# First three weight blocks multiplied k tile by k tile, the first tiles of x^T loaded from another queue, and the last rows stored in four pieces

## The chip, the cores and the metric

One core of a Trainium2 chip runs the whole program. The time is that of one execution on the device, in microseconds (us); three executions of the kernel before gave 893.09, 893.13 and 894.57, median 893.13 us. PE is the matrix engine (TensorE), PEld its weight loads, DVE is VectorE, ACT is ScalarE, POOL is GpSimd, and SP is SyncE, which here does nothing but issue transfers (DMAs). ACT and POOL can issue DMAs too.

## What is computed

A decoder trunk of two layers on 256 rows of width 2048. In each layer the normalised rows are multiplied by an input projection, four head groups work on the parts of the product, their gated outputs are put side by side and multiplied by an output projection, and the result is added to the rows. A last normalisation ends it. All in f32; cut to what matters here:

```python
def hybrid_layer(x, ...):
    h = rms_norm(x, norm_g)
    p = split_columns(jnp.einsum("bsd,de->bse", h, w_in))
    ...
    mixed = jnp.concatenate([fox, diff, moba, gla], axis=-1)
    return x + jnp.einsum("bse,ed->bsd", mixed, w_out)

def reference(x, ...):
    for l in range(DEPTH):
        x = hybrid_layer(x, l, ...)
    return rms_norm(x, final_norm_g)
```

## The kernel before

**Tiling.** The 2048 inputs of a projection are 16 k tiles of 128. Weights are cut into blocks of up to 512 columns, and a block into steps of two or four k tiles, each a tile `raw` of at most 128 x 1024 f32; there are five such buffers, so the load of a sixth waits until the first is free. To keep f32 precision at the faster matmul type fp32r, every operand is split into a high part `hi` and a remainder `lo`: ACT writes `hi` (a rounding copy of `raw`), DVE then writes `lo` = `raw` - `hi`. The transposed rows x^T are split in the same way into `hTp` (high part and remainder for each k tile, scaled by the norm's gain `ngt`). A product is three matmuls for each k tile and half of the 256 rows: high x high, low x high and high x low, summed in PSUM. A `raw` buffer is free when its last `lo` has been written.

**The order.** A planner written in Python holds a list of steps (`plan`), issues the matmuls in that order and puts the other engines' work between them by its own estimates of time. Steps 0, 1 and 2 are the first two k tiles of three blocks of layer 0 (348, 512 and 348 columns; the third sums into a PSUM tile called `side`). They alone are loaded in halves of one k tile (`HALVED = 3`, line 38; lines 1551 to 1555). Steps 3, 4 and 5 are the next two k tiles of the same blocks, steps 6 and 7 and so on those after. x^T comes in four tiles `four` of four k tiles each; of the first the k tiles 0 and 1 are loaded one at a time, 2 and 3 together (`load_x`, line 1498), and the second (k tiles 4 to 7) is issued with step 6 (line 1544), behind the load of step 5, which takes the first freed `raw` buffer.

**The start.** `load` (line 1540) issues from SP, in turn: step 0's first half, x^T's k tile 0, step 0's second half, x^T's k tile 1, both halves of step 1, x^T's k tiles 2 and 3, both halves of step 2, and steps 3 and 4. ACT issues `ngt`, then loads its table and runs a small activation (line 1892). `parts_of` (line 1609) splits a halved step k tile by k tile; `split_xt` (line 1572) splits x^T, the first k tile's high part on DVE (`xt_hi`, line 1561), the others' on ACT. `multiply` (line 1812) issues for a halved step first the six matmuls of its first k tile, then the six of its second (line 1835). Before any of this PE multiplies ones, to have its clock up.

**The end.** For the last 256 columns the sums of the upper 128 rows are finished before those of the lower. `final_rows` (line 1438) then adds the residual, sums the squares, lets POOL raise the mean square to the power -1/2 (`rf`), and scales the rows: columns 1280 and up on ACT, with a store issued by ACT, the first 1280 columns on DVE in two pieces of 640, each with a store issued by SP.

## Time and profile before

| | |
|---|---|
| median of the three runs | 893.13 us |
| the profiled execution | 892.94 us |
| its span, first to last instruction | 891.2 us |
| PE busy | 881.5 us (99%) |
| DVE, ACT, POOL busy | 662.2, 559.1, 60.0 us |
| DMA moved | 227.45 MB, mean 255 GB/s |

The profiled execution lasted 1.74 us longer than its span. PE's busy time shows where PE had work under way, not how fast it was; the DMA share is the mean over the core's 16 DMA engines, and can come out a little over 1 in a short stretch.

### The profile page before, as it was taken

To read this page: it belongs to the slowest core of one execution; us is meant where nothing else is said; L and a number is where in the kernel's file an instruction comes from. 1 tells how busy PE (TensorE), PEld (TensorE's weight loads), DVE (VectorE), ACT (ScalarE), POOL (GpSimd) and SP (SyncE) were. 2 spreads that over 40 slices of the span, in tenths; PEclk is the share of its full clock that TensorE was granted. 3 is DMA by queue.
4 is the path that set the end of the run, shared out by engine and by line. 5 is a ranking of instruction groups with operands and counts; after the bars stand their busy time and mean duration, and the time that the engine had idled before them with its cause. 6 is when DMAs were issued, how large, how long until landed. Compare 5 with 4: busy or idle time off the path is not lost.

```text
span 891.2 us, 12456 instructions
## 1 busy us (share of the span) xinstructions
PE 881.5 (99%) x4380; PEld 750.8 (84%) x4380; DVE 662.2 (74%) x943; ACT 559.1 (63%) x846; POOL 60.0 (7%) x87
## 2 busy tenths in 40 slices
PE   9999999999999999999999999999999999999996
PEld 7988889888887888888899888898888888888886
DVE  6689878878867967656679778879676788585583
ACT  7577675577646667644756876578644575693461
POOL 1010110000110000000000100110000100101000
PEclk9999999999999999999999999999999999999999
DMA  8889897747988685977798898878958978499742
GB/s 289 294 263 303 266 301 241 254 147 263 288 240 274 203 317 178 362 265 228 235 302 265 285 320 224 253 227 277 337 147 262 301 220 271 168 301 363 236 143 96
DMA packets 84142, 227.45 MB, mean 255 GB/s; under 512 B 9979, under 2 KB 30443, under 8 KB 83950
## 3 DMA queue, kind: packets, MB, share of 16 engines
q1 hardware_dynamic: 73336, 192.00, 63.9%
q0 software_dynamic: 9152, 33.03, 14.5%
q10 hardware_dynamic: 1590, 1.62, 0.5%
q8 instruction: 34, 0.56, 0.3%
q14 instruction: 30, 0.25, 0.1%
HBM read 204.06 MB, written 22.55 MB: 254 GB/s over the span
## 4 chain that ended last, share of the span: by engine, by line
PE 93%; DVE 2%; DMA 2%; issue 1%; ACT 1%; SPq 0%; POOLq 0%; POOL 0%; DVEq 0%; ACTq 0%
PE mm L466 79%; PE side L466 14%; DMA raw<-in_weights 2%; DVE lo L466 1%; DVE four L466 1%; ACT hi L466 1%; DMA far<-four 0%; DVE mTl L466 0%; ACT four L466 0%; ACT L466 0%; DVE raw L466 0%; DVE eight L466 0%; SPq L466 0%; POOLq L1984 0%; POOL rf L466 0%
## 5 line engine op out<-in xcount | busy, mean ns | idle before, releaser
L466 ACT ACTIVATE hi<-raw 128x1024 fp32r<-128x1024 f32 (+2 forms) x319 | 316.6, 1011 | 190.9 <-PE mm L466 110.2
L466 PE MATMUL mm<-hi,hTp 128*128 128x512 f32 (+1 forms) x1760 | 432.7, 381 | 1.2 <-ACT hTp L466 0.9
L466 DVE TENSOR_TENSOR lo<-raw,hi 128x1024 fp32r<-128x1024 f32 (+2 forms) x319 | 363.7, 1157 | 93.3 <-ACT hi L466 89.0
L466 PEld LDWEIGHTS mm<-hi,hTp 128*128 128x128 f32 x1760 | 321.5, 188 | 60.3 <-ACT hi L466 1.3
L466 PE MATMUL mm<-lo,hTp 128*128 128x512 f32 (+1 forms) x880 | 237.4, 380 | 0.1
L466 PEld LDWEIGHTS mm<-lo,hTp 128*128 128x128 f32 x880 | 162.4, 188 | 30.6 <-DVE lo L466 0.8
L466 PE MATMUL mm<-hi,mTh 128*128 128x512 f32 (+1 forms) x256 | 69.3, 377 | 0.0
L466 PE MATMUL mm<-lo,mTh 128*128 128x512 f32 (+1 forms) x256 | 69.0, 376 | 0.1
L466 PE MATMUL mm<-hi,mTl 128*128 128x512 f32 (+1 forms) x256 | 69.0, 376 | 0.0
L466 PEld LDWEIGHTS mm<-lo,mTh 128*128 128x128 f32 x256 | 46.2, 188 | 9.2 <-DVE lo L466 0.5
L466 PEld LDWEIGHTS mm<-hi,mTl 128*128 128x128 f32 x256 | 46.3, 188 | 8.8
L466 PEld LDWEIGHTS mm<-hi,mTh 128*128 128x128 f32 x256 | 46.0, 188 | 8.6 <-ACT hi L466 0.4
L466 ACT ACTIVATE four<-mm,rstd 128x512 f32<-128x512 f32 (+2 forms) x56 | 36.7, 667 | 26.3 <-PE mm L466 26.3
L466 POOL DMA_DIRECT2D four<-far x40 | 21.8, 546 | 444.0 <-DMA far<-four 193.5
L466 DVE STREAM_TRANSPOSE four<-four 128x1024 f32<-128x1024 f32 (+1 forms) x34 | 39.1, 1149 | 6.7 <-ACT four L466 6.3
L466 ACT ACTIVATE four<-four 128x512 fp32r<-128x512 f32 (+3 forms) x44 | 35.5, 819 | 12.6 <-DMA four<-far 8.8
L466 PEld LDWEIGHTS side<-four,four 128*128 128x128 f32 (+1 forms) x336 | 37.7, 190 | 3.9 <-issue 1.8
L466 PE MATMUL side<-four,four 128*128 128x128 f32 (+3 forms) x336 | 39.3, 281 | 0.0
L1686 POOL DMA_DIRECT2D xs<-in_weights x24 | 21.2, 900 | 169.5 <-DVE lo L466 36.2
L466 DVE TENSOR_TENSOR lo<-xs,hi 128x1024 fp32r<-128x1024 f32 x24 | 29.1, 1214 | 1.8 <-ACT hi L466 1.8
L466 ACT ACTIVATE mTh<-four 128x1024 fp32r<-128x1024 f32 x16 | 16.9, 1057 | 21.2 <-DVE four L466 21.1
L466 ACT ACTIVATE hi<-xs 128x1024 fp32r<-128x1024 f32 x24 | 25.4, 1060 | 7.1 <-PE mm L466 6.2
(146 smaller groups left out, 685.1 us busy)
## 6 DMA issues: line engine op xcount, KB each, us to landing
raw<-in_weights SPq DMA_DIRECT2D x271, 512.0 KB, 4.9
four<-far POOLq DMA_DIRECT2D x34, 512.0 KB, 6.7
far<-four SPq DMA_DIRECT2D x128, 128.0 KB, 3.9
raw<-in_weights SPq DMA_DIRECT2D x46, 348.0 KB, 5.1
xs<-in_weights POOLq DMA_DIRECT2D x24, 512.0 KB, 8.5
xs<-in_weights SPq DMA_DIRECT2D x8, 512.0 KB, 8.3
xs<-in_x SPq DMA_DIRECT2D x4, 512.0 KB
kept<-xs SPq DMA_DIRECT2D x1, 2048.0 KB, 10.6
```

Of the source, the lines that this page charges most:

```text
L466: op.do()
L1686: g_.eng.dma_start(ys[:, c], weights[at:at + P * 1024].rearrange("(p j c) -> p j c", p=P, j=2), accum_op=OP.add)
```

## The change

The loads of the first three steps are put in another order: SP issues the first halves of the three, then their second halves, then x^T's k tiles 2 and 3. ACT issues x^T's k tile 0, `ngt` and x^T's k tile 1. ACT and DVE split, and PE multiplies, in that order too: all three blocks' k tile 0, then all three's k tile 1. The high part of x^T's k tile 1 is made by DVE instead of ACT. The three `raw` buffers come free one behind the other after the last of these halves. At the end DVE scales its 1280 columns in three pieces of 320, 448 and 512 columns instead of two, each with its store.

```diff
-        for i in range(2):
-            q = slice(i * 640, (i + 1) * 640)
+        for q in (slice(0, 320), slice(320, 768), slice(768, 1280)):
             v_.tensor_scalar(xs[:, m, q], xs[:, m, q], r, None, op0=OP.mult)
             nc.sync.dma_start(rows[:, q], xs[:, m, q])
...
         if i == 0:
+            load_x(nc.scalar, 0, 1)
             nc.scalar.dma_start(ngt, norm_gt)
+            load_x(nc.scalar, 1, 2)
...
         if i < HALVED:
-            for j in range(2):
-                nc.sync.dma_start(raw[:, j * n:(j + 1) * n], src[:, j * n:(j + 1) * n])
-                if i == 0:
-                    load_x(nc.sync, j, j + 1)
+            firsts.append((raw, src, n))
+            if i + 1 == HALVED:
+                for j in range(2):
+                    for to, part, m in firsts:
+                        nc.sync.dma_start(to[:, j * m:(j + 1) * m], part[:, j * m:(j + 1) * m])
+                load_x(nc.sync, 2, 4)
         else:
             q_.move(raw, src, LOADED)
-        if i == 1:
-            load_x(nc.sync, 2, 4)
...
-        if kt == 0:
+        if kt < 2:
             v_.tensor_scalar(hT[0][:, kt], src, g, None, op0=OP.mult)
...
-        for j in (slice(0, 1), slice(1, 2)):
-            hi_of(s["hi"][:, j], s["raw"][:, j])
-            if s is plan[0]:
-                split_xt((j.start,))
-            lo_of(s["lo"][:, j], s["raw"][:, j], s["hi"][:, j])
-        loads["freed"].append(times.of(s["lo"]))
+        if s is plan[HALVED - 1]:
+            for j in range(2):
+                for z in plan[:HALVED]:
+                    hi_of(z["hi"][:, j], z["raw"][:, j])
+                    if z is plan[0]:
+                        split_xt((j,))
+                    lo_of(z["lo"][:, j], z["raw"][:, j], z["hi"][:, j])
+            loads["freed"].extend(times.of(z["lo"]) for z in plan[:HALVED])
...
         if any(s is z for z in plan[:HALVED]):
-            products.sort(key=lambda z: z[2])
+            if s is plan[HALVED - 1]:
+                for j in range(2):
+                    for z in plan[:HALVED]:
+                        for x, part in ((lh, "hi"), (ll, "hi"), (lh, "lo")):
+                            for m in range(2):
+                                matmul(z["block"]["ps"][m][:, :z["block"]["n"]], x[:, z["kts"][j], m * P:(m + 1) * P], z[part][:, j],
+                                       j == 0 and x is lh and part == "hi", False, main=True)
+            return
         products = [(*z, m) for z in products for m in range(2)]
```

The first transfers on SP's queue in the kernel before: `raw` is weights (128x348 a half of step 0 or 2, 128x512 a half of step 1, 128x696 and 128x1024 whole steps), `four` is x^T, `x2` two in a row.

```order
L1553 DMA raw<-in_weights 128x348
L1501 DMA four_118<-in_xt 128x256
L1553 DMA raw<-in_weights 128x348
L1501 DMA four_118<-in_xt 128x256
L1553 DMA raw<-in_weights 128x512 x2
L1501 DMA four_118<-in_xt 128x512
L1553 DMA raw<-in_weights 128x348 x2
L466 DMA raw<-in_weights 128x696
L466 DMA raw<-in_weights 128x1024
L466 DMA raw<-in_weights 128x696
L1501 DMA four_175<-in_xt 128x1024
```

The same place on SP now:

```order
L1557 DMA raw<-in_weights 128x348
L1557 DMA raw<-in_weights 128x512
L1557 DMA raw<-in_weights 128x348 x2
L1557 DMA raw<-in_weights 128x512
L1557 DMA raw<-in_weights 128x348
L1500 DMA four_115<-in_xt 128x512
L466 DMA raw<-in_weights 128x696
L466 DMA raw<-in_weights 128x1024
L466 DMA raw<-in_weights 128x696
L1500 DMA four_169<-in_xt 128x1024
```

Step 1's first half has moved from fifth to second place, and the two single k tiles of x^T have left this queue. The last two rows, step 5's load and x^T's second tile, keep their places.

ACT's first instructions before:

```order
L1543 DMA ngt<-in_norm_gt 128x32
L1892 ACT_TABLE_LOAD
L1892 ACTIVATE halfpow<-halfpow 128x8
L466 ACTIVATE hi<-raw 128x348 x2
L466 ACTIVATE hTp<-four_118,ngt 128x256
L466 ACTIVATE hi<-raw 128x512 x2
```

ACT's first instructions now:

```order
L1500 DMA four_115<-in_xt 128x256
L1543 DMA ngt<-in_norm_gt 128x32
L1500 DMA four_115<-in_xt 128x256
L1902 ACT_TABLE_LOAD
L1902 ACTIVATE halfpow<-halfpow 128x8
L466 ACTIVATE hi<-raw 128x348
L466 ACTIVATE hi<-raw 128x512
L466 ACTIVATE hi<-raw 128x348 x2
```

Two DMA issues stand ahead of the table load, one of them ahead of `ngt`, and the activation on k tile 1 of x^T is gone from between the copies of `raw`.

PE's matmuls behind the ones, before; `mm_165` and `mm_166` are the PSUM tiles of the first block's two halves of the rows:

```order
L466 MATMUL mm_165<-hi,hTp 128x348
L466 MATMUL mm_166<-hi,hTp 128x348
L466 MATMUL mm_165<-hi,hTp 128x348
L466 MATMUL mm_166<-hi,hTp 128x348
L466 MATMUL mm_165<-lo,hTp 128x348
L466 MATMUL mm_166<-lo,hTp 128x348
L466 MATMUL mm_165<-hi,hTp 128x348
L466 MATMUL mm_166<-hi,hTp 128x348
```

And now; `mm_179` and `mm_180` are the second block's:

```order
L466 MATMUL mm_165<-lo,hTp 128x348
L466 MATMUL mm_166<-lo,hTp 128x348
L466 MATMUL mm_179<-hi,hTp 128x512
L466 MATMUL mm_180<-hi,hTp 128x512
L466 MATMUL mm_179<-hi,hTp 128x512
L466 MATMUL mm_180<-hi,hTp 128x512
L466 MATMUL mm_179<-lo,hTp 128x512
L466 MATMUL mm_180<-lo,hTp 128x512
L466 MATMUL side_181<-hi,hTp 128x348 x4
L466 MATMUL side_181<-lo,hTp 128x348 x2
```

Behind the six matmuls of the first block's k tile 0 now stand the six of the second block's k tile 0, then the third's. Behind these 36 matmuls, from step 3 on, the order on PE is the same in both.

## Rows read from the trace of the kernel before

**Rows 1.** What PE waited for over the whole span: waiting engine and tile, what ended the wait, us in total, times, longest.

```profile
PE mm L466 <- ACT hTp L466: 0.9, 1, 0.9
PE side L668 <- PEq L1977: 0.8, 1, 0.8
PE mm L466 <- DVE hTp L466: 0.2, 1, 0.2
```

**Rows 2.** Busy time of each engine by stage: the stretch and its length, busy us (and instructions) of each engine, the granted clock, the mean busy share of the DMA engines, GB/s.

```profile
4.32:6.70 2.38, 1.44 (x6) 0.90 (x6) 0.82 (x3) 0.92 (x2) 0.00 (x0) 1.00 0.96 312
6.70:12.76 6.06, 6.06 (x31) 5.19 (x31) 4.77 (x9) 4.68 (x9) 0.00 (x0) 1.00 0.99 369
12.76:883.64 870.88, 870.63 (x4338) 743.68 (x4336) 653.79 (x922) 550.59 (x832) 56.20 (x76) 1.00 0.80 256
883.64:891.20 7.56, 0.00 (x1) 0.00 (x0) 2.21 (x6) 0.94 (x1) 0.67 (x1) 0.82 0.38 144
```

**Rows 3.** The opening in order of time: start, us, engine, line, operation, output<-input, count, and in brackets idle time before it and what ended it. SPq and ACTq rows are DMA issues. Rows with a count are several instructions run together.

```profile
0.74 0.40 SPq L1553 DMA_DIRECT2D raw<-in_weights  x1
0.75 0.41 ACTq L1543 DMA_DIRECT2D ngt<-in_norm_gt  x1
...
1.19 1.28 ACT L1892 ACT_TABLE_LOAD   x1 [1.19 <-PEq L1977]
1.19 0.42 SPq L1501 DMA_DIRECT2D four<-in_xt  x1
...
1.67 0.42 SPq L1553 DMA_DIRECT2D raw<-in_weights  x1
...
2.49 0.21 ACT L1892 ACTIVATE halfpow<-halfpow 128x8 f32<-128x8 f32 x1
...
3.37 0.49 ACT L466 ACTIVATE hi<-raw 128x348 fp32r<-128x348 f32 x1 [0.67 <-DMA raw<-in_weights]
...
3.83 0.35 DVE L466 TENSOR_SCALAR hTp<-four,ngt 128x256 fp32r<-128x256 f32 x1 [2.89 <-DMA four<-in_xt]
...
4.32 1.01 PE L466 MATMUL mm<-hi,hTp 128*128 128x348 f32 x4 [0.19 <-DVE hTp L466]
...
5.18 0.58 PE L466 MATMUL mm<-lo,hTp 128*128 128x348 f32 x2
5.73 0.49 ACT L466 ACTIVATE hi<-raw 128x348 fp32r<-128x348 f32 x1 [1.87 <-DMA raw<-in_weights]
...
6.70 1.11 PE L466 MATMUL mm<-hi,hTp 128*128 128x348 f32 x4 [0.94 <-ACT hTp L466]
6.72 1.30 ACT L466 ACTIVATE hi<-raw 128x512 fp32r<-128x512 f32 x2
7.09 1.72 DVE L466 TENSOR_TENSOR lo<-raw,hi 128x348 fp32r<-128x348 f32 x3
...
8.05 0.43 SPq L1501 DMA_DIRECT2D four<-in_xt  x1
8.08 1.08 PE L466 MATMUL mm<-hi,hTp 128*128 128x512 f32 x4
...
10.85 0.79 PE L466 MATMUL side<-hi,hTp 128*128 128x348 f32 x4
...
12.76 1.44 PE L466 MATMUL mm<-hi,hTp 128*128 128x348 f32 x8
...
14.17 0.91 ACT L466 ACTIVATE hTp<-four,ngt 128x256 fp32r<-128x256 f32 x2 [0.47 <-DMA four<-in_xt]
...
17.13 0.77 ACT L466 ACTIVATE hi<-raw 128x696 fp32r<-128x696 f32 x1
...
19.33 1.41 PE L466 MATMUL mm<-hi,hTp 128*128 128x348 f32 x8
```

**Rows 4.** DMA issues of the first 20 us, and the last row from the page, over the span: output<-input, queue, count, KB each, median us from issue to landing.

```profile
four<-in_xt SPq DMA_DIRECT2D x2, 512.0 KB, 7.1
raw<-in_weights SPq DMA_DIRECT2D x4, 174.0 KB, 5.3
raw<-in_weights SPq DMA_DIRECT2D x2, 256.0 KB, 4.3
...
ngt<-in_norm_gt ACTq DMA_DIRECT2D x1, 16.0 KB, 2.8
...
xs<-in_weights SPq DMA_DIRECT2D x8, 512.0 KB, 8.3
```

**Rows 5.** The end in order of time, in the form of rows 3, and two stretches of it in the form of rows 2.

```profile
885.35 0.94 ACT L466 ACTIVATE xs<-xs,rf 128x768 f32<-128x768 f32 x1 [4.82 <-POOL rf L466]
885.36 1.02 DVE L466 TENSOR_SCALAR xs<-xs,rf 128x640 f32<-128x640 f32 x2 [0.45 <-POOL rf L466]
885.94 0.81 SPq L1455 DMA_DIRECT2D out<-xs  x2
886.32 0.38 ACTq L1451 DMA_DIRECT2D out<-xs  x1
...
886.72:888.00 1.28, 0.00 (x0) 0.00 (x0) 0.00 (x0) 0.00 (x0) 0.00 (x0) 1.00 0.98 373
888.00:889.57 1.57, 0.00 (x0) 0.00 (x0) 0.00 (x0) 0.00 (x0) 0.00 (x0) 0.64 0.97 362
```

More of the change, by code (lines that the diff above doesn't have):

```diff
@@ L1483, in hybrid_trunk @@
         plan.append({**z, "block": b, "need": {(b["need"], b["l"], k // 4) for k in z["kts"]}})
-    xts = []
+    xts, firsts = [], []
     ys = xs.rearrange("p m d -> p (m d)").rearrange("p (c j n) -> p c j n", c=4, j=2)
@@ L1834, in multiply @@
         if any(s is z for z in plan[:HALVED]):
-            products.sort(key=lambda z: z[2])
+            if s is plan[HALVED - 1]:
[6 more added lines that the diff above has]
+            return
         products = [(*z, m) for z in products for m in range(2)]
-        if (s["first"] or s["last"]) and not any(s is z for z in plan[:HALVED]):
+        if s["first"] or s["last"]:
             products.sort(key=lambda z: z[4])
```

## The prediction

> **What bounds the kernel now.** I read first what PE waited for over the whole span [rows 1]. Three entries make 1.9 us, and one of them, the 0.8 before the first instruction, no kernel escapes. The others, 0.2 and 0.9, both wait for a high part of x^T. Then the stages [rows 2]: from 12.76 to 883.64 PE is busy for 870.63 of 870.88 us at a granted clock of 1.00, so whatever PE gains or loses before 12.76 should arrive unchanged at 883.64. There PE is done, and 7.56 us follow in which the last rows are scaled and stored. The change touches these two ends alone: the stretch up to 12.76, where step 3 begins, and the last 7.56 us. Last, both ends in order of time.
>
> In the opening [rows 3] the first block's k tile 0 is multiplied from 4.32 to 5.76 (5.18 and 0.58). Then PE stands for 0.94, until 6.70, though it has only the first block to go on with: the order wants that block's k tile 1, whose weights reach ACT at 5.73 (ACT had stood 1.87 for them), then comes ACT's 0.49 for the weights and its copy of x^T's k tile 1, behind them PE. At 6.70 the two k tiles of the first block are half done. The second k tile lasts until 8.08, 1.38 us for six matmuls of 348 columns, because PE keeps pace with `lo`. With everything there the same six cost less: block 2, of the same shape, takes 10.85 to 12.76 for both k tiles, so 0.955 each. Block 1, 512 wide, takes 8.08 to 10.85, so 1.385 each.
>
> **The change, the opening.** Nothing of PE's work is added or taken away: 36 matmuls before and after. What stands behind k tile 0 of block 0 is now k tile 0 of block 1, and only then come block 2's, and k tile 1 of all three. Call T the moment at which block 1 starts. If nothing is late behind it, step 3 starts at T + 1.385 + 0.955 + 0.955 + 1.385 + 0.955 = T + 5.635, where block 0's second k tile is now priced as block 2's, since its operands have 2.3 us more. Against 12.76 the gain is 7.125 - T.
>
> T has two conditions. PE has to be through with block 0's k tile 0: 5.76 if that starts at 4.32 as now. And block 1's weights must have landed (moment L), been copied by ACT, 0.65 (two in 1.30), and seen by PE, 0.04 (ACT's copy ends at 6.66, PE starts at 6.70): T = L + 0.69.
>
> The first condition moves a little. ACT now issues three DMAs, at 0.41 each with a pitch of 0.46 (SP's first two start at 0.74 and 1.19), so its table load starts at about 2.13 instead of 1.19, and with 1.28 and 0.21 ACT is free at about 3.64 instead of waiting until 3.37: +0.27 for the first weights' copy, which then ends at 4.13. `ngt`, issued second, goes out at 1.21; with its 2.8 from issue to landing [rows 4] it is there at 4.01, where now x^T ends the wait at 3.83. So DVE's first high part comes 0.18 later and PE starts at 4.50, and is through at 5.94. That is a cost of nothing as long as T is later, its cover being the wait for block 1's weights.
>
> L is what the trace does not show. Block 1's first half is issued second on SP, at 1.19 instead of 2.60. From below: the transfer that was issued at 1.19 landed at 3.83, x^T's k tile 0, half as large. From above: the two 256 KB halves took 4.3 in the median, which gives 5.5, and the slowest kind among the halves 5.3, which gives 6.49. The nearest row is the one with the same place in the line: step 0's second half was third of the weights and x^T tiles, issued at 1.67, and ended ACT's wait at 5.73. Block 1's half is again the third (step 0's first half and x^T's k tile 0 go out with it); it has 82 KB more, 0.26 us at 312 GB/s, and is issued 0.48 earlier. I take L = 5.75, so T = 6.44: PE stands from about 5.94 to 6.44, step 3 starts at 12.08, gain 0.68. The ends: T cannot be below 5.76, gain 1.36; with L = 6.49 it is a loss of 0.05.
>
> Is anything late behind T? Block 2's k tile 0 is wanted by PE at 7.83, its copy (0.49) must begin at 7.3, and it is issued at 1.67: even 5.3 lands it at 6.97. Block 0's k tile 1 is wanted at 8.78, issued at 2.13; 5.3 lands it at 7.43. The later ones have more room. DVE now also makes the high part of x^T's k tile 1, 0.35, in a place where it has about 1 us to spare. The wait that goes is thus replaced by a shorter one, of about 0.5, for weights instead of x^T.
>
> The Trainium skill speaks against part of this ("DMA: Bandwidth & Descriptors", section Issuing engines are not separate DMA queues): transfers issued by ACT and SP run on the same 16 DMA engines and interleave, and a second issuing engine saves only issue time. The DMA share of 0.96 before 6.70 [rows 2] agrees that these engines have no time to give. By that rule x^T's k tile 1, issued by ACT at 1.67 and not wanted before 8.78, goes partly ahead of block 1's weights; its 131 KB at 312 GB/s would make L 0.42 later, T 6.86 and the gain 0.26, which is the second rival.
>
> **The change, the end.** Of what follows 883.64, only what DVE's pieces release moves. From its start at 885.36 to SP's issue it takes 0.58 for 640 columns [rows 5]. DVE's 256-column scaling takes 0.35 [rows 3], so 320 columns are there some 0.16 earlier, an estimate along the line between these two. SP then issues at 885.78, 886.24 and 886.70 with its 0.46 pitch; ACT's stays at 886.32. The first data moved 0.78 after the first issue, at 886.72, and then the engines were busy (0.98 and 0.97) until 889.57: 1.05 MB in 2.85 us. The volume is unchanged, the start is 0.16 earlier, and the second piece follows as the first (164 KB, 0.44 us) ends. I take 0.1 of gain. Below: the pieces of 320 and 448 columns go at the 312 GB/s of the opening's short rows, and 0.39 MB then cost 0.19 more; or the last issue, 0.30 later than the present last, ends it 0.3 later. So -0.3 to +0.16. The upper 128 rows' stores go out 5.76 us earlier and touch nothing.
>
> The same page (section Rules for kernel authors) wants many small transfers put together into one; the piece of 164 KB is smaller than any store here. No row shows a 320-column store; by the rule the end loses, and the sum becomes 0.68 less up to 0.3.
>
> **Sum.** 0.68 + 0.10 = 0.78 us: the profiled execution's 892.94 would become 892.16. It lies 0.19 under the median of 893.13, on which the forecast stands: 892.35, rounded 892.4.
>
> **Rivals.** First, block 1 is there in time: the early transfers are held up by latency and not by bytes, and with two queues issuing at once block 1's half lands by 5.07. For it: the first two transfers landed 0.46 apart, just their issue pitch, 2.64 after issue. Against it: the third, issued at 1.67, took until 5.73, so 4.06. Then the gap on PE is gone, 1.36 + 0.16, 891.6.
>
> Second, the gain is swallowed: block 1's half lands after 6.2, because x^T's k tile 1 and `ngt` share the engines with it, or because it takes the 5.3 of the slow halves. PE then stands a whole us or more where it stood 0.94, and the opening comes out at 0.26 to -0.05. For it: the share of 0.96. Against it: with the 4.06 that the third transfer took, block 1's half would be there at 5.25. Time 893.0.
>
> Third, slower: the buffers. Step 0's `raw` is now free only after its second half's `lo`, behind those of blocks 1 and 2: PE wants that `lo` at 8.78 + 0.64, so about 9.2, where now it came at 7.6 (the first of the three `lo` that start at 7.09). SP's issue of step 5 waits for that, and behind it stands x^T's second tile, now issued at 8.05, then at 9.65. Step 6, at 12.08 + 6.57 = 18.65 (19.33 - 12.76), needs its copies, 0.91, and its own weights' copy behind them on ACT, 0.77: landing later than 16.97 makes PE wait, later than about 17.75 it costs the whole gain. With the 7.1 of its kind it lands at 16.75, just in time; with the 8.3 that 512 KB took elsewhere on SP at 17.95, and PE loses 0.98: 0.20 over the present time, 893.3, up to 893.7 with the worst end. Against it: now it landed at 14.17, 6.1 after issue, behind a queue of bytes (share 0.99), and with the same bytes ahead it would land near that again.
>
> That the change does not do what it says, the orders on SP, ACT and PE exclude.
>
> **How the numbers follow.** What the measurement can tell from no change is about 0.2%, 1.8 us: below 891.3 or above 894.9. The forecast (a gain of 0.4 to 1.1) has 0.55, the first rival 0.15, the second 0.20, the third 0.10. All of them lie within 0.2%. Only the first rival with an end better than I can price, or luck in the runs (one of the three before was 1.4 above the others), leaves it: faster 0.05, slower 0.03, same 0.92. The range of 891.4 to 893.7 takes in the first rival's 891.6 and the third's worst end, with 0.2 for the runs' spread below.
>
> **What would show it.** Right: block 1's 128x512 matmuls follow the first six of 348 columns, PE's wait before them is about 0.5 and is ended by ACT's copy of the weights, block 0's second k tile takes about 0.95, step 3 starts near 12.1, no new wait of PE before 883 and the last matmul near 883.0; the first store at the end is issued 0.4 after DVE's start. Wrong: a wait of 1 us or more before block 1 (second rival), none (first), or a wait at step 6 for x^T (third), or a last DMA byte later than 5.9 us after the last matmul (the end).

## The result, and the profile after

The changed kernel is slower: 899.82 us median of six runs (896.12 to 901.46) against 893.35 (893.09 to 894.57) for the kernel before on the same chip, ratio 1.0065, 95% interval 1.0044 to 1.0086. A second series on another chip gave 898.72 us (twelve runs, 896.93 to 904.33), ratio 1.0051 [1.0031, 1.0071]. Chips differ, so below each kernel is given as its ratio to the kernel before in the same session; 0.1% is 0.9 us.

The profiled execution took 896.12 us, the fastest of the six. Its span is 894.3 us, where it was 891.2. So the trace explains 3.1 us, and the other 3 or so of the median have to come from places that vary from run to run. Of the 18 executions of the changed kernel in the two series, the five with the lowest mean granted clock, 0.992 to 0.994, took 900.80 to 904.33 us, and the others, at 0.995 to 0.998, 896.12 to 900.91.

What PE waited for over the span, in the form of [rows 1]:

```profile
PE mm L466 <- ACT hi L466: 1.7, 2, 1.5
PE mm L466 <- DVE lo L466: 0.9, 1, 0.9
PE side L668 <- PEq L1987: 0.8, 1, 0.8
```

The waits for x^T's high part are gone, and others of 2.6 us stand in their place. They lie at two places, the opening and one that the prediction did not look at. First the opening, PE, in the form of [rows 3]:

```profile
5.59 1.50 PE L466 MATMUL mm<-hi,hTp 128*128 128x348 f32 x4 [1.45 <-ACT hi L466]
6.89 0.78 PE L466 MATMUL mm<-lo,hTp 128*128 128x348 f32 x2
7.47 1.91 PE L466 MATMUL mm<-hi,hTp 128*128 128x512 f32 x4
9.17 0.84 PE L466 MATMUL mm<-lo,hTp 128*128 128x512 f32 x2
9.85 0.79 PE L466 MATMUL side<-hi,hTp 128*128 128x348 f32 x4
...
14.06 1.44 PE L466 MATMUL mm<-hi,hTp 128*128 128x348 f32 x8
```

The order is the intended one, but the first matmul comes at 5.59 instead of 4.32, and six matmuls of 512 columns fill 7.47 to 9.85, 2.38 us instead of 1.385: the first four take 1.70 us, 0.43 from one start to the next, twice the 0.23 of the second block's k tile 1 later (11.74). Six of 348 columns at 9.85 take 0.95 again. Until about 9.7 PE ran at half pace. The matmuls of ones ahead of it had run at that pace too, in both kernels: their weight loads, one for each 512 columns, start 0.43 apart (1.16, 1.59, 2.01 and so on). Step 3 starts at 14.06, not 12.76. The view by stages, in the form of [rows 2], tells nothing of it; PE is busy throughout and the clock reads 1.00:

```profile
5.59:14.06 8.47, 8.47 (x36) 7.69 (x37) 6.75 (x13) 6.35 (x11) 0.00 (x0) 1.00 0.94 330
```

What was late for the first matmul, on ACT and DVE:

```profile
0.74 0.41 ACTq L1500 DMA_DIRECT2D four<-in_xt  x1
1.19 0.45 ACTq L1543 DMA_DIRECT2D ngt<-in_norm_gt  x1
1.67 0.45 ACTq L1500 DMA_DIRECT2D four<-in_xt  x1
...
4.00 0.49 ACT L466 ACTIVATE hi<-raw 128x348 fp32r<-128x348 f32 x1 [0.34 <-DMA raw<-in_weights]
4.83 0.63 ACT L466 ACTIVATE hi<-raw 128x512 fp32r<-128x512 f32 x1 [0.34 <-DMA raw<-in_weights]
```

```profile
5.09 0.35 DVE L466 TENSOR_SCALAR hTp<-four,ngt 128x256 fp32r<-128x256 f32 x1 [4.16 <-DMA ngt<-in_norm_gt]
```

PE's row names ACT, but ACT's copy for the first block was done at 4.49. The last thing to be ready was DVE's high part of x^T, at 5.44, and that had stood for `ngt`, which took 3.9 us from its issue at 1.19 where it took 2.8 [rows 4]. Both ACT copies of weights came early enough.

The second place lies between 38 and 51 us. ACT and its DMA issues there, before and after:

```profile
38.52 0.44 ACTq L466 DMA_DIRECT2D four<-in_gla_wa  x1
...
42.68 0.24 ACTq L466 DMA_DIRECT2D four<-in_gla_ba  x1
42.97 1.06 ACT L466 ACTIVATE four<-four 128x1024 f32<-128x1024 f32 x1 [3.26 <-DMA four<-in_gla_wa]
```

```profile
39.79 0.55 ACTq L466 DMA_DIRECT2D four<-in_gla_wa  x1
...
44.78 0.32 ACTq L466 DMA_DIRECT2D four<-in_gla_wa  x1
46.79 0.24 ACTq L466 DMA_DIRECT2D four<-in_gla_ba  x1
47.08 1.06 ACT L466 ACTIVATE four<-four 128x1024 f32<-128x1024 f32 x1 [6.09 <-DMA four<-in_gla_wa]
```

```profile
48.87 0.91 PE L466 MATMUL mm<-hi,hTp 128*128 128x348 f32 x4 [0.23 <-ACT hi L466]
50.64 0.59 PE L466 MATMUL mm<-lo,hTp 128*128 128x348 f32 x2 [0.86 <-DVE lo L466]
```

ACT has six small loads of constants to issue there (`gla_wa`, `gla_ba`; the last fence is PE, after). Each load has a semaphore that tells of its landing; SP's loads and ACT's take the same few in turn, and an issue waits until the load that had its semaphore before has landed. Everything behind it on ACT waits too. In the program's instruction order three of the waits read like this, in both kernels (DMAHW5 and so on are these semaphores):

```
L466 DMA four_508<-in_gla_ba 1x512 [waits DMAHW5_49]
L466 DMA four_508<-in_gla_wa 16x2x256 [waits DMAHW6_49]
L466 DMA four_508<-in_gla_ba 1x512 [waits DMAHW7_49]
```

The users before them on these semaphores are SP's weight loads, and the traces show the waiting. The load that ACT's fifth of the six issues has to wait for was issued by SP at 37.39 before and 38.67 now; time to landing, before and now:

```profile
raw<-in_weights SPq DMA_DIRECT2D x1, 348.0 KB, 3.6
raw<-in_weights SPq DMA_DIRECT2D x1, 348.0 KB, 6.1
```

It landed at 41.01 before, and ACT issued at 41.03; now at 44.76 and 44.78. SP's loads are later now: it issues x^T's third tile at 20.61 (17.87 before), its fourth at 31.55 (28.10). So ACT stands 6.09 us instead of 3.26, and PE waits 0.23 and then 0.86 behind it.

To see where time is lost over the span I compare the start of the same matmul, counted from the last one, in two profiled executions. The changed kernel is behind by 1.30 us at step 3, still 1.28 at 47 us, 2.90 at 50, 3.19 after 540 and 3.16 at the end: two steps hold nearly all. The end of the program is as long as it was: from DVE's scaling to the end of the span it takes 5.8 us (888.52 to 894.3), as before (885.36 to 891.2) [rows 5].

```profile
888.52 1.14 DVE L466 TENSOR_SCALAR xs<-xs,rf 128x320 f32<-128x320 f32 x3 [0.45 <-POOL rf L466]
```

### The profile page after: what moved, and what is told of

Its sections match the earlier page's. It is cut to its first block, busy times and chain, and to the rows that moved or that the text cites. A ratio compares the mean times of both kernels' runs of the same rounds, so it can differ in the third digit from the quotient of the medians.

```text
span 894.3 us, 12460 instructions
## 1 busy us (share of the span) xinstructions
PE 883.2 (99%) x4380; PEld 752.4 (84%) x4380; DVE 662.1 (74%) x946; ACT 558.4 (62%) x845; POOL 59.5 (7%) x87
## 4 chain that ended last, share of the span: by engine, by line
PE 92%; DMA 2%; DVE 2%; ACT 2%; issue 1%; ACTq 0%; POOLq 0%; POOL 0%; DVEq 0%; SPq 0%
PE mm L466 79%; PE side L466 13%; DMA raw<-in_weights 2%; DVE lo L466 1%; DMA four<-in_gla_wa 1%; ACT hi L466 1%; DVE four L466 1%; ACT L466 0%; ACT four L466 0%; DVE raw L466 0%; DVE mTl L466 0%; ACTq L466 0%; DVE eight L466 0%; DVE xs L466 0%; POOLq L1994 0%
```

## The experiments

My theory after the first comparison had three parts: the loads of the opening get in each other's way when two queues issue them at once; PE's gap before its first matmul lets its pace fall to half; and something in the order holds back the `raw` buffers, with them SP's loads, and with those ACT's constants. The rivals were a cost of the four-piece end, and that the new k tile order itself is dear. Each ratio rests on 6 to 12 executions. "Behind" is the comparison of starts just described, in the profiled execution, against the first profile of the kernel before. "ACT stands" is ACT's wait behind the constants near 45 us, and the last column is what PE loses between 45 and 55 us.

| kernel | ratio [95%] | behind at step 3, us | behind at 55 us | ACT stands, us | PE loses there, us |
|---|---|---|---|---|---|
| e1_ngt_first | 1.0048 [1.0032, 1.0065] | 1.54 | 3.42 | 6.37 | 1.89 |
| e2_long_warm | 1.0066 [1.0040, 1.0091] | 0.01 | 3.38 | 6.78 | 2.37 |
| e3_before_short_warm | 0.9995 [0.9981, 1.0010] | -0.44 | -0.44 | 4.37 | 0.00 |
| e4_tail_only | 0.9999 [0.9981, 1.0017] | -0.32 | 0.40 | 5.20 | 0.72 |
| x1_queue_only | 1.0027 [1.0016, 1.0038] | 2.03 | 3.03 | 5.48 | 0.99 |
| x2_order_only | 1.0036 [1.0020, 1.0051] | -0.56 | 3.57 | 6.69 | 2.21 |
| x3_after_consts_pool | 1.0012 [0.9999, 1.0025] | 1.29 | 1.29 | 1.09 | 0.00 |
| x4_before_consts_pool | 0.9991 [0.9978, 1.0003] | -0.51 | -0.51 | 1.09 | 0.00 |
| x5_order_fill | 1.0009 [0.9995, 1.0023] | -0.51 | 3.30 | 8.32 | 3.83 |
| x6_before_nofill | 1.0043 [1.0023, 1.0063] | -0.41 | 5.88 | 8.40 | 5.51 |
| x7_after_again | 1.0051 [1.0031, 1.0071] | 1.79 | 4.01 | 6.70 | 2.21 |
| x8_order_fill_pool | 0.9989 [0.9977, 1.0001] | -0.25 | -0.18 | 1.09 | 0.00 |
| y1_after_fill | 1.0020 [1.0006, 1.0034] | -0.38 | 1.24 | 6.10 | 1.62 |
| y2_after_fill_pool | 1.0001 [0.9990, 1.0012] | 1.16 | 1.10 | 1.09 | 0.00 |
| y3_nofill_pool | 1.0002 [0.9990, 1.0014] | -0.47 | 1.10 | 0.96 | 0.00 |

One trace is one execution, and the first profile of the kernel before is a quick one: 892.94 us, where the medians of its later series are 894.0 to 895.2. e4 has the code of the kernel before up to the last rows, and its trace is 0.32 ahead at step 3, 0.40 behind at 55 us and 1.77 behind at 140. So a microsecond in a single trace is no effect of an edit by itself. The last two columns do go together: PE loses nothing as long as ACT stands 4.37 us or less (3.26 in the kernel before), and beyond that what ACT stands over some 4.47, to within 0.1 us, in every trace but x6's.

### The opening: e1_ngt_first, e2_long_warm, e3_before_short_warm

In e1, `ngt` goes out first on ACT; in e2, PE multiplies ones for longer; e3 is the kernel before with fewer ones:

```diff
-            load_x(nc.scalar, 0, 1)
             nc.scalar.dma_start(ngt, norm_gt)
+            load_x(nc.scalar, 0, 1)
             load_x(nc.scalar, 1, 2)
```

```diff
-WARM = (512,) * 7 + (256,)
+WARM = (512,) * 12 + (256,)
```

```diff
-WARM = (512,) * 7 + (256,)
+WARM = (512,) * 4
```

> The changed kernel with one pair of ACT's issues exchanged: ngt first, then x^T's k tile 0. Theory A (ngt, issued second on ACT, landed 3.9 us after issue instead of 2.8, so that PE stood 1.45 us behind the ones instead of 0.18, and PE's matmuls then ran at half pace until 9.8): DVE's first high part starts near 3.9, PE's first block near 4.4, six matmuls of block 1's k tile 0 take about 1.4 instead of 2.4, and the time falls from about 899.8 to 892.3 to 893.5, with a spread of the runs under 2 us. Rival B (the k tile order itself is at fault: the first three raw buffers come free late, SP's issues and ACT's constants behind them slip, and PE is held up near 50 us): the time falls by no more than the 1.3 us of the later start, to 897 or more.

> The changed kernel with five more matmuls of ones ahead of the first block (12 of 512 columns instead of 7), so that PE has no gap to speak of before the late first block; loads are as in the changed kernel, ngt still second. Theory A: the late data still cost 1.3 us, but PE's pace is full from the first block on (0.95 for 348 columns and 1.4 for 512), the scatter of 896 to 901 goes, and the time is 893.0 to 894.8. If the pace is slow for another reason than the gap, or if B holds, the time stays at 897 to 901.

> The kernel before, loads and order untouched, with only four matmuls of ones of 512 columns instead of seven and a half, so that PE stands from about 2.5 to 4.3. Theory A: the gap alone makes it slow and scattered like the changed kernel: first matmuls of 512 columns 0.42 us apart, time 895 to 901. Rival B and every theory of the loads: nothing changes, 893.0 to 894.0.

Measured, e1: with `ngt` early it is x^T's k tile 0 that is late. DVE:

```profile
5.36 0.35 DVE L466 TENSOR_SCALAR hTp<-four,ngt 128x256 fp32r<-128x256 f32 x1 [4.43 <-DMA four<-in_xt]
```

Issued by ACT at 1.19, that tile is used at 5.36, where SP's issue at the same 1.19 had it used at 3.83 [rows 3]. PE starts at 5.86, and the ratio stays at 1.0048. So the order on ACT's queue was not the fault, and swapping two issues mends nothing: what is late is whatever stands second there. In each half microsecond from 2.5 to 5.0 us the DMA engines moved 318 to 360 GB/s in the changed kernel and 117 to 347 before. More bytes arrive, only not those that are wanted first.

e2 takes the gap away, and with it the half pace:

```profile
5.88 1.01 PE L466 MATMUL mm<-hi,hTp 128*128 128x348 f32 x4
6.74 0.58 PE L466 MATMUL mm<-lo,hTp 128*128 128x348 f32 x2
7.16 1.09 PE L466 MATMUL mm<-hi,hTp 128*128 128x512 f32 x4
```

PE starts even later than in the changed kernel, then multiplies without a wait, and step 3 comes at 12.76 as in the first profile of the kernel before. The late start alone thus takes back the 0.68 that the forecast 12.08 had promised, and the half pace costs the changed kernel 1.30 more. e2 loses another 1.0 between 18 and 23 us, around two waits of 0.2 for DVE's remainders, and its time is no better for the full pace, 1.0066: the opening's loss is not what the median shows.

e3 has a gap of 1.62 us before its first matmul at 4.26 and half pace until about 7.2, and step 3 at 12.31 all the same, since PE waits for data there anyway; its time, 0.9995, is not the 895 us or more that theory A gave it. Half pace is dear only where PE's pace sets the end of the stretch.

What brings the half pace on is not shown, and the gap alone does not explain it. In x2, x4 and x6 PE begins the first block at half pace after gaps of 0.20, 0.12 and 0.07 us; in y1 it runs at full pace after 1.30 us; in e1, x1 and x7 it begins at full pace and falls to half while it multiplies (in e1 from about 7.2 to 10.7, by the spacing of the starts). The ones run at half pace themselves, and in e2 they do so until about 5.7 us, 4.9 us after the first (by their starts, 0.43 apart). So the usual 3.4 us of ones can end before PE's clock is up, which would fit x2, x4 and x6; whether it was so in the changed kernel is not shown. e2 both closes the gap and lengthens the ones, and does not tell the two apart.

### The end: e4_tail_only

```diff
-        for i in range(2):
-            q = slice(i * 640, (i + 1) * 640)
+        for q in (slice(0, 320), slice(320, 768), slice(768, 1280)):
```

> The kernel before with the stores of the last rows in four pieces and nothing else. The prediction's term: 0.1 less, between 0.16 less and 0.3 more, so 893.0 to 893.6. Read in the profile as the time from the last matmul to the end of the span, 7.56 in the kernel before and 7.5 in the changed one by its rows.

Measured: 0.9999, no difference within 0.2%. The stores in four pieces cost nothing that can be seen, and gain nothing. From the last matmul to the end its trace takes 7.8 us, where 7.5 was expected; the traces with the stores in three pieces take 7.2 to 7.7 there, those in four 7.4 to 8.1. So the 0.1 us in question cannot be told from chance.

### The change in halves: x1_queue_only, x2_order_only

x1 is the kernel before with x^T's k tiles 0 and 1 issued by ACT behind `ngt`. x2 is the changed kernel with these two back on SP, each behind the first block's half:

```diff
             nc.scalar.dma_start(ngt, norm_gt)
+            load_x(nc.scalar, 0, 1)
+            load_x(nc.scalar, 1, 2)
...
-                if i == 0:
-                    load_x(nc.sync, j, j + 1)
```

```diff
-            load_x(nc.scalar, 0, 1)
             nc.scalar.dma_start(ngt, norm_gt)
-            load_x(nc.scalar, 1, 2)
...
+                        if to is firsts[0][0]:
+                            load_x(nc.sync, j, j + 1)
```

> The kernel before, its order of splitting and multiplying kept, but x^T's k tiles 0 and 1 issued by ACT behind ngt instead of by SP between the weights. Theory S (sharing: with nine loads in flight on two queues the first ones land late; in the exchange of ngt and x^T the k tile of x^T issued by ACT at 1.19 landed only near 5.3 instead of 3.8): PE's first block starts after 5.0 instead of 4.3, step 3 after 13.5 instead of 12.76, and the time is 895 to 899 against 893.5 to 894 before. Rival K (the k tile order and the buffers it frees late are the cause, the queue is harmless): first block at 4.3, time as before.

> The changed kernel, k tile order and stores kept, but x^T's k tiles 0 and 1 issued by SP as before, each behind the first block's half of the same k tile; ACT issues only ngt. Theory S: the first block starts near 4.3 again and the second at 6.2 to 6.6 as the prediction had it, step 3 starts near 12.1, and the time is 892 to 894. Rival K: the start is as good, yet the loads behind the first three buffers slip by a microsecond or more, ACT's constants wait longer near 45 us and PE stands there; time 895 to 899.

Measured, x1: x^T's k tile 1, issued at 1.66 by ACT, is waited for until 6.72; before, it was issued at 2.13 by SP, and ACT's copy of it began at 6.14.

```profile
6.72 0.51 ACT L466 ACTIVATE hTp<-four,ngt 128x256 fp32r<-128x256 f32 x1 [2.13 <-DMA four<-in_xt]
```

PE waits 0.72 and 0.98, runs at half pace from about 8 to 11 us, and is 2.03 behind at step 3. The second queue is a loss by itself, 1.0027; what part of it is the half pace is not separated.

x2 shows the k tile order without it:

```profile
4.34 1.50 PE L466 MATMUL mm<-hi,hTp 128*128 128x348 f32 x4 [0.20 <-DVE hTp L466]
5.64 0.78 PE L466 MATMUL mm<-lo,hTp 128*128 128x348 f32 x2
6.46 1.19 PE L466 MATMUL mm<-hi,hTp 128*128 128x512 f32 x4
...
12.20 1.12 PE L466 MATMUL mm<-hi,hTp 128*128 128x348 f32 x6
...
19.41 0.90 PE L466 MATMUL side<-lo,hTp 128*128 128x348 f32 x4 [1.10 <-DVE lo L466]
21.77 0.91 PE L466 MATMUL mm<-lo,hTp 128*128 128x348 f32 x4 [0.20 <-DVE lo L466]
```

(The last two rows are from a later stretch of the same view.) Step 3 starts 0.56 earlier than in the first profile. But that profile is late there: in e4, with the opening of the kernel before, PE's wait before the first block's k tile 1 is 0.67, not 0.94, and step 3 comes at 12.44, in x4 at 12.25:

```profile
6.40 1.11 PE L466 MATMUL mm<-hi,hTp 128*128 128x348 f32 x4 [0.67 <-ACT hTp L466]
...
12.44 1.44 PE L466 MATMUL mm<-hi,hTp 128*128 128x348 f32 x8
```

So a gain of the order at step 3 is not shown; x5 and x8, with the same order, come at 12.25 and 12.51. From there to 26 us x2 loses 1.92, with waits for DVE's remainders of weights of 1.30, and the place between 45 and 50 us takes another 2.2. An opening that is no slower ends in 1.0036.

### ACT's constants: x3_after_consts_pool, x4_before_consts_pool

The six loads of `gla_wa` and `gla_ba` are issued by POOL, in the changed kernel and, as a control, in the kernel before:

```diff
-            a_.move(w3[i:i + 16], gla_wa2.rearrange("l r e -> r l e"), CONSTANT)
...
+                give(Op("da", partial(nc.gpsimd.dma_start, to, src), [src], [to], CONSTANT))
```

> The changed kernel with six small loads of constants (gla_wa and gla_ba, near 40 us) issued by POOL instead of ACT, all else in its order. In the changed kernel ACT stood 6.09 us behind the issue of these loads (3.26 before), and PE then waited 0.23 and 0.86 for ACT's copies and DVE's remainders. Theory W (ACT's issue of these loads is held back, and the copies behind it come late): PE's waits near 49 us go, and PE is 1.6 us sooner from there on; time 1.5 to 4 under the changed kernel's 898 to 900. If the copies there were late for their data instead, the waits stay and the time too.

> The same move of the six small loads from ACT to POOL in the kernel before, the control. Theory W: in its profile PE lost nothing there, so 893.0 to 894.2, at most its late runs of 895 to 899 become rarer. If POOL's issue helps by itself, the kernel before gains as much as the changed one does.

POOL has little to do at the start and issues the six in the opening (from 4.00 to about 7.2 us in y2, below), so the edit both frees ACT and moves these 102 KB by more than 30 us; the control has the same move.

Measured: x3 is 1.29 behind at step 3 and 1.29 at 55 us; the loss between 45 and 50 is gone. Its ratio falls from 1.0051 on the same chip (1.0065 in the first series) to 1.0012, the control's only to 0.9991, whose interval takes in 1. So 0.39 to 0.53% of the changed kernel's time goes with ACT's issues at this place, and 0.09% of the kernel before, which is not clear of none. The kernel before can lose there too: e4's trace loses 0.72, though nothing is changed there. The spread shrinks as well: x3's runs reach from 894.93 to 897.74, those of x7 from 896.93 to 904.33. And the low clocks go: of the 59 executions with POOL's issues none has a mean granted clock under 0.996, and of the 95 of the kernels whose traces lose 0.99 us or more here 20 have 0.995 or less.

Something else takes 1.0 and 1.1 us in x3's and x4's traces between 80 and 93 us, and 0.9 to 1.1 in y2's and y3's, where PE waits 0.3 for a remainder of DVE's; x8's has nothing there. Since the control has it, it does not come from the change; what it is was not looked into.

### What holds the loads back: x5_order_fill, x6_before_nofill, x7_after_again, x8_order_fill_pool

The diff takes more out than it shows at first. `multiply` calls the planner (`fill`) after every six matmuls; for the first three steps the new code multiplies in a loop of its own and returns ahead of those calls. x5 is x2 with the calls put back; x6 is the kernel before with nothing but the calls left out; x7 is the changed kernel again; x8 is x5 with POOL's issues.

```diff
-                    for z in plan[:HALVED]:
+                    for n, z in enumerate(plan[:HALVED]):
+                        if j or n:
+                            loads["left"] = sum(lasts(y) for y in plan[:HALVED]) * (1 - (j * HALVED + n) / 6)
+                            fill()
```

```diff
-            if k and k % 6 == 0:
+            if k and k % 6 == 0 and not any(s is z for z in plan[:HALVED]):
```

> As the kernel with only the k tile order changed (x2_order_only: 897.92 us, 1.0036 of the kernel before), but the planner is called again between the first blocks' groups of six matmuls, so that VectorE's remainder of step 5's weights stands ahead of the second pair of x^T remainders again. My theory (the planner's calls that fell away held back the raw buffers, and with them SyncE's loads): step 3 still starts near 12.2 us (0.56 earlier than before), the waits for VectorE near 19.4 and 21.8 us (1.30 together) go, SyncE issues x^T's third tile near 18 us, not 22.2, and the loss of 1.6 near 46 to 50 us shrinks; the time lies within 2 us of the kernel before, between 893 and 896. Rival (the k tile order itself frees the raw buffers later, whatever the planner does): the loads go on being late, the waits stay, and the time is that of x2_order_only, 3 us above the kernel before. Second rival (the order of the front does not matter and the losses near 47 us are chance): the front is as in the theory, and the time is still 3 us above.

> The kernel before, with the planner's calls left out during the matmuls of the first three steps, as the change leaves them out; nothing else. My theory: step 3 starts near 12.3 to 12.8 us as before, but VectorE does four x^T remainders ahead of step 5's weight remainder, SyncE's third tile of x^T is issued later than 17.9 us (near 20), VectorE's remainders are waited for near 19 to 22 us, and ScalarE is held behind its constants near 45 us for more than 3.3 us; the time is 1 to 3 us above the kernel before. Rival (the k tile order alone frees the buffers later): SyncE's issues are as before, no new wait, and the time is within 0.5 us of the kernel before.

> The changed kernel once more, for one chip with the others. By my theory its front loses the same 1.3 us by step 3 (first block near 5.6 us after a wait of 1.4 to 1.7 us, half pace until near 9.7) and 1.6 more near 46 to 50 us behind ScalarE's constants, whatever the chip; what else it loses differs from run to run. Its ratio to the kernel before is 1.004 to 1.008. Rival (the front's loss is an accident of one execution): first block before 5.0 us, and less than 0.7 us lost by step 3.

> As x5_order_fill, with the six loads of gla_wa and gla_ba issued by GpSimd, not by ScalarE. My theory: the gain of 0.5 us at step 3 is kept through 50 us, since neither the planner's order nor ScalarE's issues of constants hold anything back; 892 to 894.5 us, the kernel before or a little less. Rival (something else near 82 to 138 us takes the gain, as in both kernels with GpSimd's issues so far, about 1 us at 82 to 93 us): 0.5 us ahead until 80 us, behind by 0.5 us or more from 93 us on, and a time 0.5 to 2 us above the kernel before.

Measured, x6: leaving out these calls alone costs 0.43%, where the whole change costs 0.51% in the same series (x7). DVE around 15 us, before and in x6:

```profile
14.87 0.87 DVE L466 SCALAR_TENSOR_TENSOR hTp<-four,ngt,hTp 128x256 fp32r<-128x256 f32 x2
15.79 1.68 DVE L466 TENSOR_TENSOR lo<-raw,hi 128x696 fp32r<-128x696 f32 x2
17.38 0.88 DVE L466 SCALAR_TENSOR_TENSOR hTp<-four,ngt,hTp 128x256 fp32r<-128x256 f32 x2
```

```profile
14.76 0.87 DVE L466 SCALAR_TENSOR_TENSOR hTp<-four,ngt,hTp 128x256 fp32r<-128x256 f32 x2
16.75 0.89 DVE L466 SCALAR_TENSOR_TENSOR hTp<-four,ngt,hTp 128x256 fp32r<-128x256 f32 x2 [1.12 <-ACT hTp L466]
17.55 0.88 DVE L466 TENSOR_TENSOR lo<-raw,hi 128x696 fp32r<-128x696 f32 x1
```

In x6 the second pair of x^T remainders stands ahead of step 5's remainder of weights, and DVE waits 1.12 for it, so the remainder comes at 17.55 instead of 15.79. Its `raw` buffer comes free that much later. SP then issues x^T's third tile at 21.23, not 17.87, and the constants on ACT read:

```profile
48.48 1.06 ACT L466 ACTIVATE four<-four 128x1024 f32<-128x1024 f32 x1 [8.40 <-DMA four<-in_gla_wa]
```

The wait near 20 us was 0.2 only, and the loss between 45 and 55 us was 5.5. ACT's 8.40 over 4.47 would make it 3.9. The rest is pace: behind PE's long wait here the clock drops to half, and the view by stages shows it, in the form of [rows 2]:

```profile
50.00:53.00 3.00, 1.88 (x9) 1.59 (x10) 2.93 (x5) 2.78 (x4) 0.00 (x0) 0.96 0.03 7
53.00:56.00 3.00, 3.00 (x11) 2.74 (x11) 1.57 (x6) 0.17 (x1) 0.91 (x2) 0.50 0.92 270
```

This is one way in which a longer wait at the constants makes an execution still longer; that the slowest executions of the changed kernel lose their time so was not profiled. The time, 0.43% or 3.8 us, is over the 1 to 3 that I expected: the mechanism held, its price was set too low.

x5: with the calls back x2's 1.0036 becomes 1.0009, and the waits near 20 us are gone, as the theory had it. SP issues x^T's third tile at 19.82, sooner than x2's 22.16 but not near 18. And its profiled execution, its slowest at 898.13 us, is 3.3 behind at 55 us. The row says what ACT waited for:

```profile
47.49 1.06 ACT L466 ACTIVATE four<-four 128x1024 f32<-128x1024 f32 x1 [8.32 <-DMA xs<-in_weights]
```

A load by SP into `xs`, which ACT's instruction does not read, ended the wait of 8.32: here the row names the load whose landing ACT's last issue had waited for. So this place is not safe with the calls either. By the ratios it goes wrong less often; the one trace does not show how often.

x7 repeats the changed kernel: PE's first wait is 2.2, longer than expected, it begins at full pace and falls to half from about 7 to 10 us, is 1.79 behind at step 3, and loses 2.2 more by 55 us. x8 has the lowest ratio here, 0.9989; its trace is 0.2 ahead of the kernel before at 80 us and still at 93, so its rival did not come true.

### Do the parts add up: y1_after_fill, y2_after_fill_pool, y3_nofill_pool

y1 is the changed kernel with x5's calls, y2 that with POOL's issues, y3 is x6 with POOL's issues. The edits are those shown above.

> The changed kernel with the planner called again between the first blocks' groups of six matmuls. My theory (the calls cost most, the two queues the rest): the front still loses 1.3 to 1.8 us by step 3, but SyncE's loads are back near the times of the kernel before plus that, and the time is 1.001 to 1.004 of the kernel before (x1_queue_only, with the queues alone: 1.0027), under the 1.0051 of the changed kernel on this chip. Rival (the calls matter only in the old k tile order): 1.005 as the changed kernel. If the two costs were independent and added, it would be 1.0051 less 0.0027 to 0.0043, 1.001 to 1.0025.

> As y1_after_fill, with the loads of gla_wa and gla_ba issued by GpSimd. My theory: PE is 1.3 to 1.8 us late at step 3, stays so to 50 us with no further loss, and the time is 1.0005 to 1.0025 of the kernel before, the front's loss alone. Rival (the late front grows elsewhere as well): over 1.003.

> The kernel before with the planner's calls left out (x6_before_nofill: 1.0043) and the loads of gla_wa and gla_ba issued by GpSimd. My theory (the late loads cost time only where ScalarE stands behind those issues): 0.4 us behind at 26 us as in x6, then nothing more to 50 us, where x6 lost 5.5; 0.999 to 1.001 of the kernel before. Rival (the late loads cost elsewhere): it loses 2 us or more between 40 and 60 us all the same, in waits for weights or remainders, and stays at 1.003 or more.

Measured: y3 is at 1.0002. Take the six issues off ACT, and the left-out calls, 1.0043 in x6, are no longer to be seen against the kernel before; against the control with POOL's issues, 0.9991, 0.1% is left, which is within the two intervals. The trace has 1.09 behind by 26 us, with waits of 1.1 near 20 us, more than the 0.4 expected, and nothing more until 80. The late loads were paid for at ACT's constants.

y1, with the calls back, is at 1.0020, y2 at 1.0001. y2's trace is 1.16 behind at step 3 and 1.10 at 55 us, so nothing is lost in between, as expected; both this and its ratio are a little under the ranges given. But the front of y1 did not lose the 1.3 to 1.8 that I had expected:

```profile
5.44 1.02 PE L466 MATMUL mm<-hi,hTp 128*128 128x348 f32 x4 [1.30 <-DVE hTp L466]
6.30 0.58 PE L466 MATMUL mm<-lo,hTp 128*128 128x348 f32 x2
6.72 1.08 PE L466 MATMUL mm<-hi,hTp 128*128 128x512 f32 x4
...
12.38 1.44 PE L466 MATMUL mm<-hi,hTp 128*128 128x348 f32 x8
```

Up to here y1 and the changed kernel have the same instructions in the same order on PE, ACT, DVE and SP. The first matmul lies 0.15 apart (5.44 and 5.59), step 3 lies 1.68 apart: y1 ran the 36 matmuls at full pace, 6.94 us, the changed kernel the first eleven at half, 8.47. At the constants ACT stands 6.10 us in y1's trace and PE loses 1.62, as much as in the changed kernel's; SP issues x^T's third tile at 19.19, not near the 17.87 of the kernel before. So it is the ratio, not this trace, that shows what the calls are worth here. The half pace is a matter of the single execution; of the profiles with the new front, both queues and the same matmuls of ones, the changed kernel's two, e1's, x3's and y2's are 1.2 to 1.8 behind at step 3, only y1's is not.

## Why the prediction was wrong

The forecast was 892.4 us and no measurable change, with 0.03 for slower. By its steps:

**T, the moment at which block 1 starts: mis-sized, and set by the other condition.** The step took L = 5.75 and T = 6.44 from the landing of block 1's weights. Its own terms, 5.73 + 0.26 - 0.48, give 5.51, and in the changed kernel ACT had these weights at 4.83: earlier than the first rival's 5.07. T came at 7.47 all the same, with no wait of PE before it, since PE was through with the first block's k tile 0 only then. x2 comes near the forecast (ACT's copy at 5.78, block 1 at 6.46, step 3 at 12.20), but there these weights are issued third on SP, at 1.67, not second at 1.19, so that is luck. "T + 5.635" holds at full pace: y1's block 1 starts at 6.72 and step 3 5.66 later. The gain was counted from 12.76, a single and late execution; from e4's 12.44 the same sum leaves 0.36 of the 0.68, and no run shows a gain of the order.

**"With its 2.8 from issue to landing it is there at 4.01": wrong.** It took 3.9 in the changed kernel, and the first matmul moved from the forecast 4.50 to 5.59. The prediction weighed the Trainium skill's rule ("DMA: Bandwidth & Descriptors", section Issuing engines are not separate DMA queues) that loads from different engines run on the same DMA engines and interleave. It charged it to block 1's weights alone, as the second rival. They were in time (4.83); the two loads that stand first in need, `ngt` and x^T's k tile 0, paid, as e1 shows by swapping them. The longer landings agree with the rule; the place was mis-chosen.

**"A cost of nothing as long as T is later": wrong, there was no cover.** Block 1's weights did not hold T, so a late start is carried on to step 3: y1 and e2, both at full pace, start 0.44 apart (5.44 and 5.88) and reach step 3 0.38 apart, e2 0.68 after the forecast. In the changed kernel half pace adds 1.30, a term that the prediction put at nothing. The Trainium skill ("TensorE: Matmul & The Clock Gate", Part 1: The HAM clock gate) says that PE runs at half rate after an idle window of about 3.4 us, and that this window runs freely, so that the moment of the switch varies. The traces agree with the varying; PE had no gap of 3.4 us in any of them, and the half pace came after gaps of 0.07 to 2.17 us, or did not come after 1.30. The view of stages that I read had 1.00 for the granted clock in those stretches, so only the spacing of matmuls shows it. Step 3 came 1.30 later than before in place of 0.68 earlier.

**"Whatever PE gains or loses before 12.76 should arrive unchanged at 883.64": the step that failed most.** It was read from PE's 870.63 busy of 870.88 us [rows 2]. That PE is never idle in one execution says that nothing was late there, not by how much. ACT stood 3.26 behind its constants without PE noticing, and the table puts the end of this slack at about 4.47: 1.2 us. SP's loads slipped by 1 to 3.5 us, ACT's wait grew to 6.09, and PE lost 1.62. x2 refutes the step by itself: no later than the kernel before at step 3, and 4.13 lost from there to 55 us, where e4 lost 0.72.

**"Is anything late behind T?": asked only up to 8.78 us, and of too little.** The steps of the prediction count what PE, ACT and the queues do in the opening. That the new code also returns ahead of the planner's calls is in the diff, and DVE's changed order behind step 3 was there to be read ahead of the run. In x6 this alone is 0.43%.

**The third rival: near in its mechanism, wrong in place and price.** That late buffers hold back SP's loads is what happened, though by the ratios the planner's missing calls are most of it (y1 has them back and is at 1.0020). It had SP's step 5 issued at 9.2 instead of 7.7 and x^T's second tile at 9.65; these came at 8.67 and 9.04. It looked for the bill at step 6 and put it at 0.2 to 0.6 us. At step 6 (20.62) PE did not wait. The slip was carried on from buffer to buffer and paid 28 us later, at 1.6 us in the profile; 3.5 to 4.7 in the medians (0.39 to 0.53%) go when ACT no longer issues the constants there.

**The end: within its range, its gain not shown.** 0.10 was forecast; the first store was issued 0.41 after DVE's start, as said, but the two profiles take the same 5.8 us, and the spread of the traces there is 0.5 us and more.

**The sum, from the runs.** With POOL's issues, where the constants hold nothing back, the changed kernel with its calls (y2) is 0.10% above the control (x4): about 0.9 us for the opening, against 1.1 in y2's trace. The left-out calls add 0.11% there (x3 over y2), and the rest of the 0.51 to 0.65% is ACT's constants. Each of these differences has an uncertainty of 0.1 to 0.2%, so only the constants' part is clear of noise; that the other two cost anything in the median is not shown. The two queues' share by itself I have as 0.27% (x1) in the old k tile order and 0.11% (y1 over x5, on two chips) in the new; which holds was not settled. Nor was it tried to give ACT's constants semaphores of their own while ACT still issues them: that the wait is for the semaphore is read from the order of instructions, from x5's row and from issues that follow the landing by 0.02 us. What the experiments show is that the loss goes when ACT no longer issues the constants at that time.

A version clearly better than the kernel before was not found. x8 is at 0.9989 [0.9977, 1.0001], but the control x4 without any of the change is at 0.9991, and neither is clear of 1: the k tile order brings nothing that can be measured.

## What to carry to other kernels

An engine that is never idle shows no slack: before a gain at the start is carried to the end, look for the places where another engine or a queue waits long without the bound engine noticing (here ACT's 3.26 us behind six tiny loads), for a slip of a microsecond in what feeds them can surface there, larger. Where a planner orders the work, a loop that is rewritten also moves the planner's calls; compare the order on every engine some way beyond the edit. A second issuing queue at the start can make what is needed first arrive later, though more bytes arrive in all (here `ngt` by 1.1 us). And a gain that is counted from one trace is no surer than that trace: look how far the same moment moves in another execution (here step 3 by 0.3 to 0.5 us).

## What the hardware showed that I had not expected

- A DMA issue on ACT can be held for microseconds by a load that another engine issued, by way of a semaphore that both use: ACT issued at 44.78, 0.02 us after a load of SP's had landed, and stood 6.09 in all (the changed kernel; 8.32 in x5). It works the other way too: in the changed kernel SP's sixth load went out at 4.17, 0.02 after ACT's x^T k tile 0 had landed.
- What PE loses can follow another engine's wait to within 0.1 us, from a threshold on: nothing up to 4.37 us of ACT's wait, then all that is over some 4.47.
- The 3.4 us of ones ran at half pace themselves, nearly or quite to their end, and the first block came at full or at half pace after them, with no order by the gap between (half after 0.07 in x6, full after 1.30 in y1). The profile's column for the granted clock read 1.00 either way at the start, and 0.50 in a half-pace stretch later (x6, 53 to 56 us).
- `ngt`, 16 KB, took 2.8 us from issue to landing when it was the first on ACT's queue, and 3.9 when x^T's k tile 0 stood ahead of it; x^T's k tile 0 was used 2.6 us after SP's issue and 4.2 after ACT's, both issued at 1.19.
